# Loading and splitting the per layer input earlier in the second down stage

## The chip, the cores and the metric

The kernel runs on one core of a Trainium2 chip, in one launch. The metric is the time of one execution in device microseconds (us). A core has five engines with queues of their own: TensorE (PE, matmuls, with its weight loads PEld), VectorE (DVE), ScalarE (ACT), GpSimd (POOL) and SyncE (SP). Here SP only issues DMAs, and POOL issues those DMAs that add into a buffer (`accum_op`).

## The reference

```python
for i in range(DEPTH):                                    # 2 layers
    h = h + 0.5 * swiglu(rmsnorm(h, norm_ffn1[i]), ffn1_w_gate[i], ffn1_w_up[i], ffn1_w_down[i])
    hn = rmsnorm(h, norm_mix[i])
    h = h + (ab_mixer(hn, ...) if i % 2 == 0 else c_mixer(hn, ...))
    h = h + 0.5 * swiglu(rmsnorm(h, norm_ffn2[i]), ffn2_w_gate[i], ffn2_w_up[i], ffn2_w_down[i])
    gate = sigmoid(rmsnorm(h, norm_ple[i]) @ w_ple_gate[i])
    h = h + gate * (p[i] @ w_ple_proj[i])                 # per layer input
return rmsnorm(h, norm_final)
```

The sequence has 512 positions, the model 1024 features, the inner width of SwiGLU is 2816, and the per layer input `p[i]` has 512 x 256 values. All are float32.

## The kernel before

Every float32 operand of a matmul is split into a high part and a low part of the type that PE takes: `split` (L153 to L155) lets ACT copy the high part (L154) and DVE subtract it for the low part (L155). A product of two such operands is three matmuls: high by high, high by low, low by high. `split_chunk` splits one 128x512 chunk into two `act` tiles, `parts` a weight buffer `wr` of up to 128x1024 into `wh` and `wl`.

Each layer has two SwiGLU blocks, `ffn(i, 1, ...)` and `ffn(i, 2, ...)`. Each ends with a down stage, `down` (from L493), so there are four in the program; the second one of a layer is followed by the stage of the per layer input, `ple`. A down stage multiplies the 512 x 2816 inner values by the 2816 x 1024 weights with seven block products in place of eight (a scheme of Strassen's kind). In the code the products are called "first" to "seventh", without order of time, and each is cut into six steps s = 0 to 5 along the inner width (step 0 has one unit of 128, the others two). "sixth 3" below is step 3 of the product called sixth. A step of two units is 12 matmuls of 128x512. PE adds up each product in its own PSUM banks: the seventh in `tr` banks, first and sixth in `mm`, second and fourth in `mm` and `ob`, fifth and third in `sc`.

The order of the steps is a list written out by hand (`order`): first a phase of second, first and fifth steps, which ends at index 13; then seventh 0, second 5, first 5, fifth 4, seventh 1, sixth 0, seventh 2, fifth 5, sixth 1, seventh 3, fourth 0, sixth 2, seventh 4, fourth 1, sixth 3, seventh 5, fourth 2, sixth 4, fourth 3, third 0, and so on. For each index the program does four things:

```python
product(*step)          # the matmuls on PE
after(*step)            # what belongs behind this product
ahead(i + LEAD + 1)     # prepare (the splits) four steps ahead, load (DMAs) seven steps ahead
```

`prepare` of a seventh step has DVE add two weight blocks (L566), then ACT and DVE make `wh` and `wl`, and then, in steps 3 to 5, the parts of the inner sums; and it has POOL add a further block to the same buffer by a DMA (L547), which a sixth step reads later, as a fourth step reads what a sixth one left. `load` issues the weights on SP: wide ones into `wr` (5 buffers, L520), narrow ones into `tmp` (10 buffers, L526).

Within this stage the instructions are pinned (`put`): each engine executes them in the order in which they are written. `ffn` hands `down` a function that calls `per_layer` (L478 to L482) twice, once for each half of 128 features: it loads 128x512 values of `p[i]` into a `tmp` buffer by SP (L481) and splits them. `after` calls it behind the product fourth 0 (L653), so the splits stand ahead of the preparation of sixth 3 on ACT and DVE. The four parts are read by `ple`, some 40 us later. In the first down stage of a layer nothing is handed over, and the code is otherwise the same.

Of the kernel before, what the change touches and what calls it, by code (L numbers as in the profile page):

```python
# [56 lines left out]
class Trunk:  # L57
# [92 lines left out]
    def put(self, ins):  # L150
        return self.tc.keep_in_program_order(ins) if self.pinned else ins
# [302 lines left out]
    def ffn(self, i, which, k_next):  # L454


        nc, io = self.nc, self.io
        gu, dn = io[f"gu{which}"][i], io[f"dn{which}"][i]
        first = i == 0 and which == 1
        kept = io["xT"].rearrange("p c t -> c p t") if first else self.put_away()  # L460
        a, sums = [], [None] * K2
        rows, t = self.front(gu, first)
        y = self.xg

        def between():
            a.extend(self.turn_back(rows, self.tbank))
            for k in range(READY):
                if 2 * k + 2 <= len(a) and sums[k] is None:
                    sums[k] = self.inner_sums(*a[2 * k:2 * k + 2])

        for j in range(BLOCKS):
            n = 4 * UNIT + j * 8 * UNIT
            rows = self.block(gu[:, n:n + 8 * UNIT], y, t, between, first and j == 0)
        self.begin_norm(k_next)
        p = lambda: [self.per_layer(i, c) for c in range(2)]
        self.down(dn, a, sums, kept, p if which == 2 else None, lambda n: a.extend(self.turn_back(rows, self.tbank, n)))

    def per_layer(self, i, c):  # L478

        raw = self.tmp()  # L480
        self.nc.sync.dma_start(raw, self.io["pT"][i, :, c, :])  # L481
        return self.split_chunk(raw, self.nc.vector)  # L482

    def inner_sums(self, a, b):

# [7 lines left out]
    def down(self, w, a, sums, kept, inner, turn):  # L493

        nc, H = self.nc, T // 2
# [6 lines left out]
        n = len(units)  # L502
        r1, r2, r3 = [self.bank(), self.bank()], [self.bank(), self.obank()], [self.sbank(), self.sbank()]
        rb = rc = c11 = c5 = c2 = u3 = c21 = None
        x1, x2, x3, x4, raws, more, ops = ({} for _ in range(7))
        put = self.put
# [91 lines left out]
        def copied(p):  # L598
            out = [self.act() for _ in p]
            for o, x in zip(out, p):  # L600
                put(copy(o, x, AF.Copy))
            return out
# [18 lines left out]
        def first_half(m):  # L621
            p, h = self.tbank(), hs[m]
            turned(p[:, l], c11, m)
            turned(p[:, r], c21, m)
            put(nc.vector.scalar_tensor_tensor(h, p, 0.5, h, op0=ALU.mult, op1=ALU.add))
            self.h[m] = h
            floating(self.norm_split, m)

        def second_half(m, x, c):
            p = self.tbank()  # L630
            for j in range(2):
                turned(p[:, j * H:(j + 1) * H], x, m - M + j)
            for j in range(2):
                h = hs[m + j]
                put(nc.vector.scalar_tensor_tensor(h[:, c], p[:, j * H:(j + 1) * H], 0.5, h[:, c], op0=ALU.mult, op1=ALU.add))
                self.h[m + j] = h
            for j in range(2):
                floating(self.norm_split, m + j, c)

        def after(kind, s):  # L640
            nonlocal rb, rc, c11, c5, c2, u3, c21
            if (kind, s) in (("first", 2), ("fifth", 1)):
                turn(range(2) if kind == "first" else range(2, 4))
                if kind == "fifth":
                    rb = [self.tbank(), self.tbank()]
            elif (kind, s) == ("first", 5):
                c11 = copied(r1)
                for o, p in zip(c11, r2):
                    put(tt(o, p, o, op=ALU.add))
                rc = [self.bank(), self.obank()]  # L650
            elif (kind, s) == ("fifth", 5):
                c5 = copied(r3)
            elif (kind, s) == ("fourth", 0) and inner:  # L653
                self.p = inner()
            elif (kind, s) == ("first", 3):
                hs.extend(self.act() for _ in range(KC))
                for m in range(KC):
                    nc.sync.dma_start(hs[m], kept[m])
            elif (kind, s) == ("sixth", 5):
                c2, u3 = copied(r1), [self.act(), self.act()]  # L660
                for i in range(2):
                    put(tt(u3[i], c2[i], rb[i], op=sub))
                for i in range(2):
                    put(tt(c5[i], c5[i], u3[i], op=sub))
            elif (kind, s) == ("fourth", 5):
                c21 = [self.act(), self.act()]
                for i in range(2):
                    put(tt(c21[i], rc[i], u3[i], op=ALU.add))
                second_half(M + 2, c5, r)
            elif (kind, s) == ("third", 2):  # L670
                second_half(M, c5, r)
            elif kind == "third" and 2 < s < 5:
                first_half(2 * s - 6)
                first_half(2 * s - 5)
# [14 lines left out]
        for i, step in enumerate(order):  # L689
            product(*step)  # L690
            after(*step)
            ahead(i + LEAD + 1)
# [941 lines left out]
```

## Time and profile before

| what | us |
|---|---|
| median of 3 runs | 2001.87 (2001.15 to 2005.03) |
| the profiled execution | 2003.01 |
| its span, first to last instruction | 2001.2 |
| matmuls of the second down stage of layer 0 | from 857 to 975 |
| matmuls of the second down stage of layer 1 | from 1815 to 1933 |

The profile shows one execution. Its page gives the busy time of each engine; the views of the trace give each engine's instructions in order of time, with the idle time before them and what ended it, the waits summed up, and the busy time in chosen stretches with the clock that PE was granted (1.00 is full speed). A row of the timeline merges neighbours of one kind (x8). A line such as L154 is that of a helper, so an instruction is recognised by its buffers: `act<-tmp` of L154 is the high part of the per layer input.

### The profile page before, as it was taken

How to read it: one execution, taken by the hardware profiler on the slowest of the kernel's cores; microseconds unless marked ns; L12 is line 12 of the kernel's file. 1: busy time of each engine (PE TensorE's matmuls, PEld its weight loads, DVE VectorE, ACT ScalarE, POOL GpSimd, SP SyncE). 2: the span in 40 equal slices, each digit the busy share in tenths (PEclk: the TensorE clock that was granted, in tenths of full speed). 3: DMA queues.
4: the chain of work that ended last, by engine and by line, in shares of the span. 5: the costliest groups of instructions: out<-in, count | busy, mean ns of one | idle time of the engine just before them, and what ended most of it. 6: DMA issues, size and time to landing. Idle time of an engine off the chain costs nothing.

```text
span 2001.2 us, 28069 instructions
## 1 busy us (share of the span) xinstructions
PE 1974.6 (99%) x9702; PEld 1644.8 (82%) x9702; DVE 1551.5 (78%) x2716; ACT 1218.5 (61%) x2107; POOL 334.7 (17%) x390
## 2 busy tenths in 40 slices
PE   9999999999999999999999999999999999999998
PEld 7888887879888888887888888888888888888786
DVE  8787888698767677787786778887888768678785
ACT  7555656477645555565565556655766556657553
POOL 1111111341211212011122120111000122111111
PEclk9999999999999999999999999999999999999999
DMA  9877697543426777779468785894343577768961
GB/s 275 195 200 163 182 232 229 131 96 80 101 64 226 174 179 183 173 213 252 150 219 184 175 193 153 216 247 150 103 133 101 179 189 189 170 147 229 251 194 42
DMA packets 152223, 348.24 MB, mean 174 GB/s; under 512 B 26512, under 2 KB 34192, under 8 KB 152080
## 3 DMA queue, kind: packets, MB, share of 16 engines
q1 hardware_dynamic: 112128, 235.23, 35.4%
q0 software_dynamic: 39808, 111.17, 31.3%
q8 instruction: 76, 1.25, 0.2%
q14 instruction: 67, 0.55, 0.1%
q10 hardware_dynamic: 144, 0.04, 0.0%
HBM read 318.06 MB, written 17.27 MB: 168 GB/s over the span
## 4 chain that ended last, share of the span: by engine, by line
PE 60%; issue 6%; DVE 6%; DMA 5%; ACT 2%; POOL 1%; SPq 0%; DVEq 0%; POOLq 0%; ACTq 0%
PE mm L179 5%; PE mm L181 5%; PE mm L180 5%; PE mm L595 5%; PE mm L369 4%; PE mm L370 4%; PE mm L368 4%; PE sc L595 3%; DMA wr<-in_gu_dram 3%; PE sc L370 2%; PE sc L369 2%; PE sc L368 2%; DVE wl L155 2%; PE ob L595 2%; PE sc L181 1%
## 5 line engine op out<-in xcount | busy, mean ns | idle before, releaser
L154 ACT ACTIVATE wh<-wr 128x1024 fp32r<-128x1024 f32 (+1 forms) x428 | 438.4, 1029 | 412.1 <-PE mm L370 87.3
L155 DVE TENSOR_TENSOR wl<-wr,wh 128x1024 fp32r<-128x1024 f32 (+1 forms) x428 | 509.8, 1195 | 176.5 <-ACT wh L154 168.0
L368 PE MATMUL mm<-wh,act 128*128 128x512 f32 x640 | 251.0, 392 | 0.0
L370 PE MATMUL mm<-wh,act 128*128 128x512 f32 x640 | 250.8, 392 | 0.0
L369 PE MATMUL mm<-wl,act 128*128 128x512 f32 x640 | 249.5, 390 | 0.1
L179 PE MATMUL mm<-act,wh 128*128 128x512 f32 (+1 forms) x472 | 185.0, 394 | 0.4 <-ACT act L154 0.4
L181 PE MATMUL mm<-act,wl 128*128 128x512 f32 (+1 forms) x472 | 184.6, 392 | 0.0
L180 PE MATMUL mm<-act,wh 128*128 128x512 f32 (+1 forms) x472 | 183.9, 390 | 0.0
L154 ACT ACTIVATE wh<-tmp 128x512 fp32r<-128x512 f32 x248 | 144.9, 623 | 63.8 <-PE sc L370 32.7
L595 PE MATMUL mm<-wh,act 128*128 128x512 f32 x528 | 159.5, 397 | 6.3 <-ACT wh L154 6.3
L155 DVE TENSOR_TENSOR wl<-tmp,wh 128x512 fp32r<-128x512 f32 x248 | 160.5, 684 | 2.9 <-ACT wh L154 2.5
L155 DVE TENSOR_TENSOR act<-act,act 128x512 fp32r<-128x512 f32 (+1 forms) x268 | 141.2, 554 | 3.9 <-ACT act L154 3.7
L338 POOL DMA_DIRECT2D wr<-in_gu_dram x80 | 79.5, 996 | 376.9 <-DVE wl L155 373.4
L369 PEld LDWEIGHTS mm<-wl,act 128*128 128x128 f32 x640 | 120.2, 188 | 24.9 <-DVE wl L155 0.7
L370 PEld LDWEIGHTS mm<-wh,act 128*128 128x128 f32 x640 | 120.2, 188 | 24.4
L368 PEld LDWEIGHTS mm<-wh,act 128*128 128x128 f32 x640 | 120.3, 188 | 23.8
L154 ACT ACTIVATE act<-act 128x512 fp32r<-128x512 f32 (+1 forms) x268 | 125.8, 513 | 15.0 <-DVE act L312 8.3
L368 PE MATMUL sc<-wh,act 128*128 128x512 f32 x320 | 124.7, 390 | 0.5 <-DVE act L292 0.5
L370 PE MATMUL sc<-wh,act 128*128 128x512 f32 x320 | 124.7, 390 | 0.0
L369 PE MATMUL sc<-wl,act 128*128 128x512 f32 x320 | 124.6, 389 | 0.0
L595 PEld LDWEIGHTS mm<-wh,act 128*128 128x128 f32 x528 | 100.3, 190 | 27.9 <-ACT wh L154 7.2
L547 POOL DMA_DIRECT2D wr<-in_dn_dram x72 | 62.3, 880 | 358.4 <-DVE wl L155 352.8
(260 smaller groups left out, 4316.3 us busy)
## 6 DMA issues: line engine op xcount, KB each, us to landing
wr<-in_gu_dram SPq DMA_DIRECT2D x92, 512.0 KB, 4.9
tmp<-in_gu_dram SPq DMA_DIRECT2D x160, 256.0 KB, 3.6
wr<-in_gu_dram POOLq DMA_DIRECT2D x80, 512.0 KB, 7.7
tmp<-in_dn_dram SPq DMA_DIRECT2D x132, 256.0 KB, 6.1
wr<-in_dn_dram POOLq DMA_DIRECT2D x60, 512.0 KB, 7.6
tmp<-in_gu_dram POOLq DMA_DIRECT2D x80, 256.0 KB, 6.0
wr<-in_dn_dram SPq DMA_DIRECT2D x40, 512.0 KB, 5.6
act<-kept SPq DMA_DIRECT2D x56, 256.0 KB, 4.6
```

The lines of the kernel that those rows point to most:

```text
L154: self.put(self.nc.scalar.activation(hi, src, AF.Copy))
L155: self.put((lo_eng or self.nc.vector).tensor_tensor(lo, src, hi.bitcast(F32), op=ALU.subtract))
L179: mm(out, stat[0], mov[0], start=start, stop=False)
L180: mm(out, stat[0], mov[1], start=False, stop=False)
L181: return mm(out, stat[1], mov[0], start=False, stop=stop)
L338: nc.gpsimd.dma_start(raw, q[:, u * UNIT:(u + 1) * UNIT], accum_op=ALU.add)
L368: mm(p, xh, wh, start=start and k == 0, stop=False, skip_group_check=True)
L369: mm(p, xh, wl, start=False, stop=False, skip_group_check=True)
L370: self.last_mm = mm(p, xl, wh, start=False, stop=stop and k == half - 1, skip_group_check=True)
L547: put(nc.gpsimd.dma_start(raw, b[:, u.start * T:u.stop * T], accum_op=ALU.add))
L595: put(nc.tensor.matmul(p, x[k][a][:, c], w[b][:, j * T:(j + 1) * T], start=start and k == a == b == 0, stop=stop and b == 1 and k == u.sto ...
```

## The change

```diff
@@ ffn
         self.begin_norm(k_next)
-        p = lambda: [self.per_layer(i, c) for c in range(2)]
-        self.down(dn, a, sums, kept, p if which == 2 else None, lambda n: a.extend(self.turn_back(rows, self.tbank, n)))
-
-    def per_layer(self, i, c):
-
-        raw = self.tmp()
-        self.nc.sync.dma_start(raw, self.io["pT"][i, :, c, :])
-        return self.split_chunk(raw, self.nc.vector)
+        inner = lambda c: io["pT"][i, :, c, :]
+        self.down(dn, a, sums, kept, inner if which == 2 else None, lambda n: a.extend(self.turn_back(rows, self.tbank, n)))
@@ down, after
             elif (kind, s) == ("fifth", 5):
                 c5 = copied(r3)
-            elif (kind, s) == ("fourth", 0) and inner:
-                self.p = inner()
+            elif (kind, s) == ("fifth", 2) and inner:
+                for c in range(2):
+                    more["inner", c] = self.tmp()
+                    put(nc.sync.dma_start(more["inner", c], inner(c)))
+            elif (kind, s) == ("seventh", 0) and inner:
+                self.p = [self.split_chunk(more.pop(("inner", c)), nc.vector) for c in range(2)]
```

The loads are issued behind the product fifth 2 (index 10) and the splits behind seventh 0 (index 14), where before both stood behind fourth 0 (index 24). The lines behind it move by 6 (the rest of `down`) or 2 (all that follows). The order on PE and on POOL stays as it was; on ACT, DVE and SP these instructions move, in both layers alike. The rows below are of layer 0.

On ACT, ahead of seventh 1 (`wh_8941` before, `wh_8953` now), the program before:

```order
L154 ACTIVATE act_8907<-act_8726 128x512
L154 ACTIVATE wh_8923<-wr_8671 128x1024
L154 ACTIVATE wh_8941<-wr_8872 128x1024
L154 ACTIVATE wh_8958<-wr_8753 128x512
L601 ACTIVATE act_8975<-mm_8481 128x512
```

and the changed one:

```order
L154 ACTIVATE act_8911<-act_8726 128x512
L154 ACTIVATE wh_8927<-wr_8671 128x1024
L154 ACTIVATE act_8943<-tmp_8842 128x512
L154 ACTIVATE act_8947<-tmp_8844 128x512
L154 ACTIVATE wh_8953<-wr_8876 128x1024
L154 ACTIVATE wh_8970<-wr_8753 128x512
L595 ACTIVATE act_8987<-mm_8481 128x512
```

The two splits stand between the `wh` of fifth 4 and that of seventh 1. On DVE their low parts stand in the same way between the `wl` of fifth 4 and the adds of seventh 1.

On ACT, between fourth 1 (`wh_9154`) and sixth 3 (`wh_9182`), the program before:

```order
L154 ACTIVATE wh_9154<-wr_8872 128x1024
L154 ACTIVATE act_9158<-act_7210 128x256
L154 ACTIVATE act_9161<-act_7224 128x256
L154 ACTIVATE act_9172<-tmp_9170 128x512
L154 ACTIVATE act_9178<-tmp_9176 128x512
L154 ACTIVATE wh_9182<-wr_8990 128x1024
L154 ACTIVATE wh_9201<-wr_9130 128x1024
```

and the changed one:

```order
L154 ACTIVATE wh_9166<-wr_8876 128x1024
L154 ACTIVATE act_9170<-act_7210 128x256
L154 ACTIVATE act_9173<-act_7224 128x256
L154 ACTIVATE wh_9182<-wr_9002 128x1024
L154 ACTIVATE wh_9201<-wr_9142 128x1024
```

The splits are gone from here; `wh_9201` is that of seventh 5. On DVE the low parts are gone from the same place.

On SP, the loads before, from the last hidden state (`kept`) over first 5 (`wr_8828`) to seventh 1 (`wr_8872` with two `tmp`):

```order
L658 DMA act_8805<-kept_6550 128x512
L520 DMA wr_8828<-in_dn_dram 128x1024
L520 DMA wr_8872<-in_dn_dram 128x1024
L526 DMA tmp_8874<-in_dn_dram 128x512
L526 DMA tmp_8875<-in_dn_dram 128x512
```

and those of the changed program:

```order
L656 DMA act_8805<-kept_6550 128x512
L514 DMA wr_8828<-in_dn_dram 128x1024
L650 DMA tmp_8842<-in_pT_dram 128x512
L650 DMA tmp_8844<-in_pT_dram 128x512
L514 DMA wr_8876<-in_dn_dram 128x1024
L520 DMA tmp_8878<-in_dn_dram 128x512
L520 DMA tmp_8879<-in_dn_dram 128x512
```

The two loads pass the weights of seventh 1 to seventh 5, which is 15 loads. At the old place, behind seventh 5, the eight `tmp` loads of the third product that follow now stand without them.

## The prediction

> **What bounds the kernel now.** I read the page first, for the share of each engine:
>
> ```profile
> span 2001.2 us, 28069 instructions
> ...
> PE 1974.6 (99%) x9702; PEld 1644.8 (82%) x9702; DVE 1551.5 (78%) x2716; ACT 1218.5 (61%) x2107; POOL 334.7 (17%) x390
> ```
>
> TensorE (PE) is busy for 99% of the span, so only two things can change the time much: an idle PE, or a PE that runs below its clock. Work moved on another engine counts only where PE waits for it. So the second view is the waits of PE, longest first (us in total, times, longest):
>
> ```profile
> PE mm L595 <- ACT wh L154: 6.3, 2, 3.3
> PE tr L1465 <- ACT tmp L1459: 1.6, 1, 1.6
> ```
>
> The largest wait of PE happens twice, in the down matmuls of L595, for a high part `wh` made by ScalarE (ACT) at L154. The third view, the timeline of PE, places it: once in the second down stage of layer 0 and once in that of layer 1. Columns are start, length, what, count, and in brackets the idle time before with its releaser.
>
> ```profile
> 921.54 1.98 PE L595 MATMUL tr<-wh,act 128*128 128x512 f32 x8
> 923.36 1.07 PE L595 MATMUL tr<-wl,act 128*128 128x512 f32 x4
> ...
> 926.76 0.39 PE L595 MATMUL ob<-wl,act 128*128 128x512 f32 x1
> 930.49 2.75 PE L595 MATMUL mm<-wh,act 128*128 128x512 f32 x8 [3.34 <-ACT wh L154]
> ...
> 938.46 0.39 PE L595 MATMUL mm<-wh,act 128*128 128x512 f32 x1
> ...
> 1884.92 0.39 PE L595 MATMUL ob<-wl,act 128*128 128x512 f32 x1
> 1888.32 3.78 PE L595 MATMUL mm<-wh,act 128*128 128x512 f32 x8 [3.00 <-ACT wh L154]
> ...
> 1896.67 0.39 PE L595 MATMUL mm<-wh,act 128*128 128x512 f32 x1
> ```
>
> Two things are to be seen. A group of 8 equal matmuls is followed after 1.82 us (921.54 to 923.36), so one takes 0.227 us. The group of 8 behind the wait takes 2.75 and 3.78 us instead of 1.98: PE is idle first and then slow. The clock is in the windows (after the five busy times: granted clock, DMA share, GB/s):
>
> ```profile
> 920.00:925.00 5.00, 5.00 (x24) 4.14 (x23) 5.00 (x10) 2.62 (x6) 0.87 (x1) 1.00 1.06 300
> ...
> 930.00:935.00 5.00, 4.51 (x13) 3.34 (x14) 3.48 (x5) 2.37 (x4) 0.86 (x1) 0.67 1.04 369
> ...
> 1890.00:1895.00 5.00, 5.00 (x14) 3.91 (x14) 3.74 (x7) 4.10 (x8) 1.54 (x2) 0.57 1.05 329
> ```
>
> Ahead of the wait 24 matmuls go into 5 us at clock 1.00; behind it 13 and 14, at 0.67 and 0.57. So the price of the place is the wait plus the slow stretch. From the start of the product sixth 3 to that of fourth 2 lie two products (sixth 3 and seventh 5), 24 matmuls, 24 x 0.227 = 5.44 us at full rate. The slot of the first was 926.76 + 0.23 = 926.99, and fourth 2 starts at 938.46: 11.47 us, 6.03 too many. In layer 1: 1885.15 to 1896.67 is 11.52, 6.08 too many. **Together 12.1 us**; 3.50 + 3.17 = 6.7 of it idle, 5.4 slow.
>
> Why was ACT late? Its own timeline:
>
> ```profile
> 921.91 0.71 ACT L154 ACTIVATE act<-act 128x256 fp32r<-128x256 f32 x2
> 925.66 0.63 ACT L154 ACTIVATE act<-tmp 128x512 fp32r<-128x512 f32 x1 [3.04 <-DMA tmp<-in_pT_dram]
> 928.86 0.63 ACT L154 ACTIVATE act<-tmp 128x512 fp32r<-128x512 f32 x1 [2.57 <-DMA tmp<-in_pT_dram]
> 929.39 1.04 ACT L154 ACTIVATE wh<-wr 128x1024 fp32r<-128x1024 f32 x1
> ...
> 1884.08 0.63 ACT L154 ACTIVATE act<-tmp 128x512 fp32r<-128x512 f32 x1 [3.77 <-DMA tmp<-in_pT_dram]
> 1886.69 0.63 ACT L154 ACTIVATE act<-tmp 128x512 fp32r<-128x512 f32 x1 [1.98 <-DMA tmp<-in_pT_dram]
> ```
>
> ACT has nothing else to wait for: it is free at 922.6, stands in front of the two splits of the per layer input until 925.66 and 928.86, and only then makes the `wh` that PE waits for. These loads were issued barely before:
>
> ```profile
> 915.61 0.97 SPq L481 DMA_DIRECT2D tmp<-in_pT_dram  x2
> ...
> DMA to landing us min/median/max: 9.3/10.7/12.7
> ```
>
> **The change, part by part.** The instruction count is unchanged: four loads, four ACT and four VectorE (DVE) splits, in two layers, move earlier; PE's and POOL's orders stay.
>
> *Removed from the old place.* ACT's two waits and two splits go (922.6 to 929.4 in layer 0), so `wh` of sixth 3 can be started at 922.6 and is done at 923.7, more than 3 us ahead of its slot at 926.99. The idle time then goes, and, if it caused the slow clock, that too: 12.1 us.
>
> *Is anything else late there?* The first down stage of each layer is the same code without the per layer input. There the same two products run so:
>
> ```profile
> 298.97 1.98 PE L595 MATMUL mm<-wh,act 128*128 128x512 f32 x8
> ...
> 303.67 0.73 PE L595 MATMUL tr<-wh,act 128*128 128x512 f32 x2 [0.20 <-DVE act L155]
> ...
> 305.16 0.39 PE L595 MATMUL mm<-wh,act 128*128 128x512 f32 x1
> ...
> 1321.87 1.98 PE L595 MATMUL mm<-wh,act 128*128 128x512 f32 x8
> ...
> 1327.72 0.40 PE L595 MATMUL mm<-wh,act 128*128 128x512 f32 x1
> ```
>
> 6.19 and 5.85 us instead of 5.44: a loss of 0.75 and 0.41 us in seventh 5, which waits for low parts by DVE (303.67). That is what is late next.
>
> *Added at the new place.* The splits now stand between fifth 4 and seventh 1:
>
> ```profile
> 892.33 1.06 ACT L154 ACTIVATE wh<-wr 128x1024 fp32r<-128x1024 f32 x1 [0.62 <-ACT act L154]
> 896.77 1.58 ACT L154 ACTIVATE wh<-wr 128x1024 fp32r<-128x1024 f32 x2 [3.39 <-DVE wr L566]
> ...
> 1856.13 1.58 ACT L154 ACTIVATE wh<-wr 128x1024 fp32r<-128x1024 f32 x2 [4.32 <-DVE wr L566]
> ```
>
> On ACT two splits of 0.63 fit into idle time of 3.39 and 4.32 us: nothing. DVE has no such gap:
>
> ```profile
> 894.18 1.22 DVE L155 TENSOR_TENSOR wl<-wr,wh 128x1024 fp32r<-128x1024 f32 x1
> 895.32 1.29 DVE L566 TENSOR_TENSOR wr<-wr,tmp 128x512 f32<-128x512 f32 x2
> ...
> 902.50 1.98 PE L595 MATMUL tr<-wh,act 128*128 128x512 f32 x8
> ```
>
> Two low parts of the size of the adds (the pair took 1.29) put off the adds of seventh 1 by up to 1.29 us, and its `wh` from 896.77 to 898.1, done by 899.2; PE wants it at 902.50. So no wait there, but DVE runs nearly without gaps from here on, and carries the delay to seventh 5.
>
> *What the delay costs at seventh 5.* The rows of layer 1:
>
> ```profile
> 1881.94 0.75 DVE L155 TENSOR_TENSOR act<-act,act 128x256 fp32r<-128x256 f32 x2
> ...
> 1889.44 1.29 DVE L566 TENSOR_TENSOR wr<-wr,tmp 128x512 f32<-128x512 f32 x2
> ...
> 1890.90 1.06 ACT L154 ACTIVATE wh<-wr 128x1024 fp32r<-128x1024 f32 x1 [2.63 <-DVE wr L566]
> ...
> 1894.07 0.68 DVE L155 TENSOR_TENSOR act<-act,act 128x512 fp32r<-128x512 f32 x1
> ```
>
> Seventh 5 needs its second low part at its seventh matmul, 6 x 0.227 = 1.36 us in; that part ends 1894.75 - 1890.90 = 3.85 us behind the start of `wh`. In the new program DVE goes on at 1882.69 (plus the delay) with `wl` of sixth 3 (1.15), the adds (1.29), and `wh` starts 0.15 later: 1885.3 without delay, so PE could start at 1885.3 + 3.85 - 1.36 = 1887.8, and it comes at 1885.15 + 2.72 = 1887.87. No wait without delay, 1.2 us with all of 1.29. I take a delay of 1.0 (DVE still has a few gaps of some tenths), so 0.9 us. In layer 0 the same sum from 925.0 gives 930.1 against 929.71: 0.4 us without delay, 1.7 with all. There seventh 4 waits for its transfer anyway,
>
> ```profile
> 917.47 0.69 DVE L566 TENSOR_TENSOR wr<-wr,tmp 128x512 f32<-128x512 f32 x1 [1.35 <-DMA tmp<-in_dn_dram]
> ```
>
> and that gap takes up most of the delay: I take 0.4 of delay, 0.8 us. Both: 1.7 us, between 0.4 and 2.9.
>
> *The loads.* They are issued behind the last load of the first products:
>
> ```profile
> 871.07 6.03 SPq L520 DMA_DIRECT2D wr<-in_dn_dram  x2
> ```
>
> The first of these two issues is at 871.07; the second ends at 877.10, having waited for its buffer. The new loads stand between them, so their 0.97 us of issue falls into a wait and delays nothing. They have from 871.4 to 893.4, 22 us, against 12.7 for the slowest such load. What they hold, two of ten `tmp` buffers for 25 us, costs nothing as the order is built: the weight loads from there up to seventh 5 wait only for a transfer eight places before them, none for a `tmp` buffer. At the old place two later weight loads move up in their stead, so the transfers stay as dense there as before (share 1.06).
>
> **Sum.** 12.1 - 1.7 = 10.4 us less (9.2 to 11.7), against the profiled execution's 2003.01 us (span 2001.2): 1992.6. That execution lies 1.1 above the median of 2001.87, inside the runs' spread. From the median: **1991.5 us**.
>
> **Rivals.**
>
> *The slow clock is not the wait's doing.* For the wait as cause: 0.67 and 0.57 stand right behind the two longest waits, the window ahead has 1.00, and the same products in the first down stages, with little wait, run at full pace. Against: the trace cannot show these two places without the wait. If the slow stretch stayed in both layers, 12.1 - 5.4 - 1.7 = 5.0 us are gained: 1996.9. If only layer 1's stayed (6.08 - 3.17 = 2.9): 1994.4. The Trainium skill, page "TensorE: Matmul & The Clock Gate", section "Part 1: The HAM clock gate (the "warmup" mystery)", says that the array falls to half rate after at least one idle window of about 3.4 us; taken strictly, layer 1's 3.00 us would be too short and its slow stretch would have another cause, which gives the 1994.4. By that rule the trace agrees for layer 0 within a tenth and differs for layer 1, where 3.00 us of idle were followed by 0.57; here the measurement decides. 5%.
>
> *Transfers become the wait.* In favour: share 1.04 to 1.06 of the DMA engines there, and a stage made 5 us shorter wants the same bytes in less time. Against: the first down stages, without the splits, lost only 0.75 and 0.41. If weights land 1 to 2 us later for seventh 5 or fourth 3 in each layer, PE waits 2 to 4 us more in all: 1993.5 to 1995.5. 14%.
>
> *It doesn't do what it says:* the loads are held up and ACT waits at the new place for as long as at the old. Then 2001.9. Against: 22 us of lead. 3%.
>
> *Slower.* Place: ACT in front of `wh` of seventh 1. ACT is in order, so a late load holds everything behind it. PE wants seventh 1 at 902.50, so `wh` has to start by 901.4 and the second load to land by 900.2, 29 us behind its issue. From there each us is a us of PE idle, and from about 3 us of idle on the slow clock comes with it (2.5 to 2.9 us). At 33 us the old price is reached again; at 36 it is 3 us more in each layer, 2008. With 12.7 as the slowest, 2%.
>
> **How the numbers follow.** Forecast 76%; late transfers 14%, clock 5%, no effect 3%, slower 2%. The forecast's own range is 2001.87 - 11.7 = 1990.2 to 1992.7, with about 1 us for a median: 1989 to 1993.5. To hold 8 in 10 with the transfers' case in part: **1989.0 to 1994.5**. A measurement of this kernel tells 0.2%, 4 us, from no change. Faster by more than that takes in the forecast, the transfers and the clock, 95%; 2 of them go to no change, since a clock that stays slow in both layers ends within 1 us of the bound. So faster 0.93, the same 0.05, slower 0.02.
>
> **What would show it.** Right: no wait of ACT for in_pT_dram in the second down stages; no wait of PE for `wh` at L595; the clock at 1.00 across both; sixth 3 to fourth 2 in 5.4 to 6.6 us; ACT's idle time ahead of seventh 1 about 1.2 shorter. Wrong: idle time of PE over 2 us at seventh 5 or later (transfers), a clock below 1.00 without an idle PE ahead of it (clock), or ACT waiting for in_pT_dram ahead of seventh 1 (slower).

## The result and the profile after

| | median us | executions | ratio to before, 95% interval |
|---|---|---|---|
| before | 2001.82 (1998.11 to 2005.03) | 12 | |
| after | 1994.51 (1991.43 to 1998.70) | 12 | 0.9965 [0.9955, 0.9975] |

The change makes the kernel 7.3 us faster, 0.35%. The forecast was 1991.5, 10.4 us less, and its range of 1989.0 to 1994.5 ends just short of the measured median. What was said of the old place came true; the size did not, for losses that the sum had no term for. The profiled execution of after took 1992.47 us, one of the shorter ones, so the pair of profiles shows 10.5 us, more than the medians do.

The page of after, its span and the share of each engine:

```profile
span 1990.7 us, 28067 instructions
...
PE 1969.4 (99%) x9702; PEld 1641.3 (82%) x9702; DVE 1552.9 (78%) x2716; ACT 1220.1 (61%) x2107; POOL 335.0 (17%) x390
```

The waits of PE in after, longest first (us in total, times, longest):

```profile
PE tr L1463 <- ACT tmp L1457: 1.6, 1, 1.6
PE tr L127 <- DVE R L124: 1.3, 1, 1.3
PE tr L608 <- DVE act L629: 1.2, 3, 0.4
```

The largest wait of before, 6.3 us for `wh` in two pieces, has left the list (its line would now be L589). The third row was 0.7 us in two pieces before, both in the first down stages: PE's transposes at the end of a down stage now wait for VectorE (DVE) more often. The timeline of PE in after at the two places, sixth 3, seventh 5 and the start of fourth 2:

```profile
925.32 1.98 PE L589 MATMUL mm<-wh,act 128*128 128x512 f32 x8
...
928.04 2.38 PE L589 MATMUL tr<-wh,act 128*128 128x512 f32 x8
...
931.19 0.39 PE L589 MATMUL mm<-wh,act 128*128 128x512 f32 x1
...
1878.57 1.98 PE L589 MATMUL mm<-wh,act 128*128 128x512 f32 x8
...
1883.41 0.74 PE L589 MATMUL tr<-wh,act 128*128 128x512 f32 x2 [0.20 <-DVE act L155]
...
1884.92 0.39 PE L589 MATMUL mm<-wh,act 128*128 128x512 f32 x1
```

From sixth 3 to fourth 2 it is 5.87 and 6.35 us, 0.43 and 0.91 above the 5.44 of full rate, where before lost 6.03 and 6.08. What is left is the wait for a low part in seventh 5 that the prediction named. The windows behind the places have the clock at 1.00 (0.67 and 0.57 before):

```profile
930.00:935.00 5.00, 5.00 (x23) 4.09 (x22) 5.00 (x9) 3.73 (x8) 0.87 (x1) 1.00 1.05 262
...
1885.00:1890.00 5.00, 5.00 (x24) 4.12 (x23) 4.20 (x8) 2.54 (x6) 0.87 (x1) 1.00 1.05 275
```

But something new stands at the end of the second down stages, in both layers. The timeline of PE in after, its transposes there:

```profile
959.07 0.63 PE L608 MATMUL tr<-ident,act 128*128 128x128 f32 x4 [0.42 <-DVE act L629]
...
962.63 0.66 PE L608 MATMUL tr<-ident,act 128*128 128x128 f32 x4 [0.19 <-DVE act L619]
...
1912.86 0.63 PE L608 MATMUL tr<-ident,act 128*128 128x128 f32 x4 [0.42 <-DVE act L629]
...
1916.43 0.66 PE L608 MATMUL tr<-ident,act 128*128 128x128 f32 x4 [0.17 <-DVE act L619]
```

In the profile of before PE has no such wait in that part of the two stages.

**A ledger of the stage.** PE's order is the same in all these kernels, so a stretch can be counted in matmuls and its time compared from kernel to kernel. Three stretches lose time in the second down stages: (a) the 53 matmuls up to the slot of sixth 3, seventh 4 among them (11.79 us for 52 in layer 0, 12.01 for 53 in layer 1 at full rate); (b) the 25 from there to the start of fourth 2 (5.67 us); (c) the last 74 of layer 0 and 75 of layer 1 (14.88 and 15.09 us, the least that any profile has). The rest of the two stages is equal to within 0.1 us everywhere. Loss in us, layer 0 / layer 1, from the starts of the matmuls in each trace:

| kernel | (a) seventh 4 | (b) sixth 3, seventh 5 | (c) stage end | sum |
|---|---|---|---|---|
| before | 0 / 0 | 6.03 / 6.08 | 0.01 / 0.01 | 12.1 |
| before, second profile (e1) | 0 / 0 | 5.90 / 5.68 | 0 / 0.04 | 11.6 |
| after | 0 / 0 | 0.42 / 0.91 | 0.79 / 0.83 | 3.0 |
| after, second profile (e2) | 0 / 4.00 | 0.07 / 0.33 | 0.77 / 0.43 | 5.6 |
| after, third profile (e13) | 0 / 0.57 | 0.04 / 0.99 | 0.84 / 0.96 | 3.4 |
| e3 loads alone | 0 / 0 | 1.60 / 0.95 | 0.47 / 0.93 | 3.9 |
| e4 splits later | 0 / 0 | 0.06 / 0 | 1.97 / 1.37 | 3.4 |
| e5 before, held | 2.39 / 2.39 | 2.22 / 2.22 | 0.01 / 0.01 | 9.2 |
| e6 after, held | 3.01 / 5.34 | 1.02 / 0.33 | 0 / 0 | 9.7 |
| e7 low parts in a gap | 0 / 0 | 0 / 0 | 0.63 / 0.71 | 1.3 |
| e8 narrow loads first | 0 / 0 | 0.17 / 0 | 0.50 / 0.55 | 1.2 |
| e9 before, narrow loads first in these stages | 0 / 0 | 5.63 / 4.69 | 0.01 / 0.01 | 10.3 |
| e10 after, the same | 0 / 0 | 0 / 0 | 0.56 / 0.47 | 1.0 |
| e11 after, the same in the first stages alone | 0 / 0 | 0.06 / 0.91 | 0.85 / 0.57 | 2.4 |
| e12 both | 0 / 0 | 0 / 0 | 0.01 / 0.04 | 0.1 |
| e14 after, the same for seventh 4 alone | 0 / 0 | 0 / 0.11 | 0.53 / 0.67 | 1.3 |

Two profiles of before lose 11.9 us on average, three of after 4.0: 7.9 us, which is what the medians of all executions give (2001.76 of 93, 1993.94 of 22, on several chips: 7.8). So the change's effect lies in these stages, and the missing 2.5 us too: in columns (a) and (c), for which the forecast had nothing. The rest of the program differs by 2.8 us between the two profiles of before and by 4.1 between those of after, with means 1.1 us apart: scatter, of the size of what is sought. The agreement to 0.1 us is therefore partly luck.

### The profile page after: what moved, and what is told of

Same layout as the page of the kernel before. It is cut to its first block, busy times and chain, and to the rows that moved or that the text cites. A ratio compares the mean times of both kernels' runs of the same rounds, so it can differ in the third digit from the quotient of the medians.

```text
span 1990.7 us, 28067 instructions
## 1 busy us (share of the span) xinstructions
PE 1969.4 (99%) x9702; PEld 1641.3 (82%) x9702; DVE 1552.9 (78%) x2716; ACT 1220.1 (61%) x2107; POOL 335.0 (17%) x390
## 4 chain that ended last, share of the span: by engine, by line
PE 77%; issue 8%; DVE 7%; DMA 4%; ACT 2%; POOL 1%; DVEq 0%; POOLq 0%; ACTq 0%
PE mm L589 7%; PE mm L369 6%; PE mm L368 6%; PE mm L370 6%; PE mm L179 5%; PE mm L181 5%; PE mm L180 5%; PE sc L589 4%; PE sc L368 3%; PE sc L370 3%; PE sc L369 3%; DVE wl L155 3%; PE ob L589 2%; DMA wr<-in_gu_dram 2%; PE tr L589 2%
## 5 line engine op out<-in xcount | busy, mean ns | idle before, releaser
L589 PE MATMUL mm<-wh,act 128*128 128x512 f32 x528 | 156.9, 391 | 0.0
L589 PEld LDWEIGHTS mm<-wh,act 128*128 128x128 f32 x528 | 99.1, 188 | 20.4
```

The lines of the kernel that those rows point to most:

```text
L589: put(nc.tensor.matmul(p, x[k][a][:, c], w[b][:, j * T:(j + 1) * T], start=start and k == a == b == 0, stop=stop and b == 1 and k == u.sto ...
```

## The experiments

**Twice the same, e1 and e2.** The kernel before and the changed one, unedited, for a second profile of each.

> The kernel before, unchanged, for a second profile. In the first profile the place (sixth 3 to fourth 2) lost 6.03 us in layer 0 and 6.08 in layer 1. Theory A (the profile was a usual execution): again 11 to 13 us over both layers, the clock at half for 3 to 7 us in each. Theory B (the size of the loss changes from one execution to the next, which is why the medians differ by 7.3 us where the profiles differ by 10.5): 8 to 10 us over both layers, with less slow clock. Time between 1998 and 2005 us.

> The changed kernel, unchanged, for a second profile. In its first profile (1992.5 us) the place lost 0.43 + 0.91 us and the end of the stage 1.3 us. Theory A (as the first profile): the same within 1 us, and a time of 1992 to 1995. Theory C (some executions have a further loss of 3 to 6 us that the first profile does not show, since three of twelve took 1998.5 to 1998.7): where this execution is above 1996 its profile shows an idle or slow PE of that size somewhere else. No wait of ScalarE for the per layer input under any theory.

Measured: before 2003.25 us (11 executions), ratio 1.0008 [0.9999, 1.0017]; after 1994.21 (5), ratio 0.9962 [0.9948, 0.9976]. Both profiles taught something. In that of before, the timeline of PE in layer 0 shows the same wait, but another rate behind it:

```profile
930.38 2.11 PE L595 MATMUL mm<-wh,act 128*128 128x512 f32 x8 [3.21 <-ACT wh L154]
...
934.59 2.07 PE L595 MATMUL tr<-wh,act 128*128 128x512 f32 x6 [1.19 <-ACT act L154]
...
938.35 0.39 PE L595 MATMUL mm<-wh,act 128*128 128x512 f32 x1
```

and the window has the clock at 1.00:

```profile
930.00:935.00 5.00, 3.43 (x14) 2.47 (x14) 3.48 (x5) 2.37 (x5) 0.87 (x1) 1.00 1.05 364
```

No slow stretch here, and yet the place lost 5.90 us instead of 6.03: PE ran sixth 3 at full rate and then stood 1.19 us more, waiting for the parts of seventh 5, which ScalarE (ACT) and VectorE make behind the same late splits. The slow clock in the first profile had mostly filled time that PE would have waited. (In layer 1 of e1 the clock did fall, to 0.66 from 1890 to 1895, and the place lost 5.68 us.) So "6.7 idle and 5.4 slow" were not two prices that add up; the place was set by the chain of ACT and VectorE behind the late load.

The profile of after, at 1999.21 us the longest of its five executions, shows what the first one did not have, at seventh 4 of layer 1. On DVE the second add of that step waits for its narrow load (`tmp`):

```profile
1874.31 0.69 DVE L560 TENSOR_TENSOR wr<-wr,tmp 128x512 f32<-128x512 f32 x1 [0.44 <-DMA tmp<-in_dn_dram]
1877.03 0.69 DVE L560 TENSOR_TENSOR wr<-wr,tmp 128x512 f32<-128x512 f32 x1 [2.03 <-DMA tmp<-in_dn_dram]
```

and on PE sixth 2, seventh 4 and the start of fourth 1:

```profile
1874.54 1.98 PE L589 MATMUL mm<-wh,act 128*128 128x512 f32 x8
...
1879.52 3.67 PE L589 MATMUL tr<-wh,act 128*128 128x512 f32 x8 [2.10 <-ACT act L154]
...
1883.95 0.39 PE L589 MATMUL mm<-wh,act 128*128 128x512 f32 x1
```

9.41 us for 24 matmuls instead of 5.44: 2.10 idle, and the group of 8 slow behind it. The two narrow loads were issued together:

```profile
1864.50 1.06 SPq L520 DMA_DIRECT2D tmp<-in_dn_dram  x2
```

so the later one landed some 12 us behind its issue. Of the 22 executions of after in all, 4 lie between 1998.5 and 1999.2, and the other 18 between 1991.3 and 1995.3.

**One half of the change each, e3 and e4.** e3 keeps the early loads and leaves the splits at the old place; e4 keeps the loads at the old place and puts the splits later.

```diff
 (e3)
-            elif (kind, s) == ("seventh", 0) and inner:
+            elif (kind, s) == ("fourth", 0) and inner:
                 self.p = [self.split_chunk(...)]
 (e4)
-            elif (kind, s) == ("fifth", 2) and inner:
+            elif (kind, s) == ("fourth", 0) and inner:
                 for c in range(2): ...
-            elif (kind, s) == ("seventh", 0) and inner:
+            elif (kind, s) == ("third", 0) and inner:
                 self.p = [self.split_chunk(...)]
```

> The loads issued behind fifth 2 as in the changed kernel, the splits left behind fourth 0 as in the kernel before. Theory 1 (ScalarE waited for late loads, the splits themselves are cheap): no wait of ScalarE for the per layer input, clock 1.00, the place loses 2.5 to 3.5 us over both layers since the two low parts (1.29 us) stand right ahead of sixth 3 and seventh 5 on VectorE; time 1 to 2 us above the changed kernel. Rival 2 (it is the place of the splits that counts): the place still loses over 8 us, time as before.

> The loads issued behind fourth 0 as in the kernel before, the splits put off to behind third 0, some 22 us later. Theory 1: no wait for the loads, no split ahead of seventh 5, so the place loses only what the first down stages lose (0.4 to 0.8 us in each layer), clock 1.00; at the end of the stage VectorE has 1.29 us more to do than in the changed kernel, so the waits of TensorE for the last additions grow from 1.3 us to 1.5 to 3 over both layers; time within 1.5 us of the changed kernel. Rival 2 (early loads are what counts): ScalarE still waits for the loads, at third 2, by 2 us or more.

Measured: e3 1995.22 us (7 executions), 0.9971 [0.9961, 0.9982]; e4 1996.47 (11), 0.9971 [0.9962, 0.9980]. Either half keeps most of the gain, and in neither does ACT wait for the per layer input: the price of before was ACT and DVE standing in front of loads that had just been issued, and not the splits' work. What differs is where DVE's work comes out (columns b and c). In e3 it comes out at seventh 5, from the timelines of DVE and, below it, of PE in layer 0:

```profile
917.95 0.69 DVE L560 TENSOR_TENSOR wr<-wr,tmp 128x512 f32<-128x512 f32 x1 [1.25 <-DMA tmp<-in_dn_dram]
...
925.40 1.29 DVE L155 TENSOR_TENSOR act<-tmp,act 128x512 fp32r<-128x512 f32 x2
```

```profile
930.83 2.08 PE L589 MATMUL tr<-wh,act 128*128 128x512 f32 x6 [0.39 <-ACT act L154]
933.11 0.73 PE L589 MATMUL tr<-wh,act 128*128 128x512 f32 x2 [0.20 <-DVE act L155]
```

In e4 nothing is lost there, and the end of the stage pays, on PE's timeline:

```profile
961.28 0.33 PE L608 MATMUL tr<-ident,act 128*128 128x128 f32 x1 [0.48 <-DVE act L666]
961.88 0.33 PE L608 MATMUL tr<-ident,act 128*128 128x128 f32 x1 [0.27 <-DVE act L666]
962.63 0.63 PE L608 MATMUL tr<-ident,act 128*128 128x128 f32 x4 [0.42 <-DVE act L629]
...
966.20 0.66 PE L608 MATMUL tr<-ident,act 128*128 128x128 f32 x4 [0.19 <-DVE act L619]
```

1.97 us against 0.79 in after: the two low parts, 1.29 us of DVE, come out almost whole. Two expectations were missed: the place lost less than the 0.4 to 0.8 us in each layer, and the median is 2.3 us above that of after in e2, on the same chip, where 1.5 was the limit. The ledger of the one profile, 3.4 us, doesn't show why. From here the theory was: with PE's pause gone, DVE has no slack left from seventh 1 to the stage's end, and a delay of DVE, from splits or from a late load, reaches PE. It holds up to seventh 5; what sets the stage's end in after is another thing, shown further below.

**A delay of one size in both kernels, e5 and e6.** Six adds on a spent buffer, 4.2 us of DVE by their rows (3.6 in the expectation), between the two adds of seventh 4 in the second down stages.

```diff
                     put(tt(z, z, y, op=ALU.add))
+                    if inner and s == 4 and j == 0:
+                        for _ in range(6):
+                            put(tt(y, y, y, op=ALU.add))
```

> The kernel before, with six extra VectorE adds of 128x512 (0.6 us each, on a spent buffer) between the two adds of seventh 4, in the second down stage of both layers: 3.6 us of VectorE, as if that step's second narrow load landed late. Theory 'the old wait took up such delays': ACT and VectorE stand waiting for the per layer input until 925.66 and 928.86 anyway, so seventh 4 comes about 3 us late on PE and sixth 3 not at all: within 1 us of the kernel before in all (2001 to 2003.5). Rival 'a late load costs the same in both kernels': 3 us and more in each layer, 2008 or later.

> The changed kernel with the same six adds in both layers. Theory: nothing behind takes up the delay now. Seventh 4 has a slack of about 0.4 us on VectorE (in the run that lost 4.0 us in layer 1 VectorE was held 2.5 us and PE idled 2.10), so about 3.2 us of PE idle in each layer, with or without a slow clock behind it (up to 2.9 each): 2000 to 2006, all of the change's gain. Rival 'slack elsewhere takes it up': within 2 us of the changed kernel, 1994 to 1996.

Measured: e5 2000.61 us (11), ratio 0.9994 [0.9985, 1.0003]; e6 2000.32 us (11), ratio 0.9996 [0.9987, 1.0004]. The delay costs the kernel before nothing that can be measured, and takes from the changed one all of its gain, some 6 us. The held kernels lose nothing at the stage end, either of them (column c). PE's timeline in e5, layer 0: the wait of 3.34 us has become two of about 1 us, at seventh 4 and seventh 5, and the wait for the per layer input is gone because its loads had time to land:

```profile
922.05 2.08 PE L598 MATMUL tr<-wh,act 128*128 128x512 f32 x6 [1.18 <-ACT act L154]
...
932.43 2.07 PE L598 MATMUL tr<-wh,act 128*128 128x512 f32 x6 [1.00 <-ACT act L154]
```

And in e6, both layers:

```profile
922.78 2.07 PE L592 MATMUL tr<-wh,act 128*128 128x512 f32 x6 [1.80 <-ACT act L154]
...
1880.57 3.67 PE L592 MATMUL tr<-wh,act 128*128 128x512 f32 x8 [3.44 <-ACT act L154]
```

e6 lies in the theory's band; e5 is within 1 us of before on its chip, 0.4 below the band in figures. In layer 0 of e6 the idle time was 1.80 us instead of 3.2; why is not shown.

**DVE's backlog, e7.** The low parts go behind the adds of seventh 1, where DVE waits 1.26 us for ACT's `wh` anyway.

```diff
-            elif (kind, s) == ("seventh", 0) and inner:
-                self.p = [self.split_chunk(more.pop(("inner", c)), nc.vector) for c in range(2)]
@@ prepare, seventh
+                if inner and s == 1:
+                    self.p = [(self.act(F32R), self.act(F32R)) for c in range(2)]
+                    for c in range(2):
+                        put(copy(self.p[c][0], more["inner", c], AF.Copy))
                 for j, y in enumerate(more.pop(s)):
                     ...
+                if inner and s == 1:
+                    for c in range(2):
+                        put(tt(self.p[c][1], more.pop(("inner", c)), self.p[c][0].bitcast(F32), op=sub))
                 w, x = self.parts(raws[n + s]), x3
```

> The changed kernel, with the two low parts of the per layer input on VectorE behind the adds of seventh 1, where VectorE waits 1.26 us for ScalarE's wh of that step in any case; the two high parts stay ahead of that wh on ScalarE. Theory 'VectorE's backlog is carried to seventh 5 and to the stage end': 1.3 us less backlog, so the losses at seventh 5 (0.43 and 0.91) go to 0.1 to 0.4 each and those at the end of the stage (0.79 and 0.81) to 0.3 or less: 1 to 2.5 us faster than the changed kernel, 1992 to 1993.4. Rival 'the stage end loses by something else, the transposes' own order': no change there, under 0.7 us gained in all.

Measured: 1992.33 us (5 executions, 1990.12 to 1992.45), ratio 0.9952 [0.9939, 0.9964]. Seventh 5 loses nothing any more (0.42 and 0.91 in after). The stage end fell only to 0.63 and 0.71, more than the 0.3 expected. So the splits account for the loss at seventh 5, and for a small part of that at the end.

**The transfers, e8.** The narrow loads of a seventh step are issued ahead of its wide one, which waits for a buffer on SP and holds them up.

```diff
-                raws[n + s], more[s] = wide(b12, u), narrow(b22, u)
+                more[s], raws[n + s] = narrow(b22, u), wide(b12, u)
```

> The changed kernel, with the two narrow loads of each seventh step issued ahead of its wide one instead of behind it, in all four down stages. In the run of the changed kernel that lost 4.0 us at seventh 4 of layer 1, the second narrow load landed some 12 us behind its issue. Theory 'some executions lose about 4 us to that late load': the narrow loads are issued some 4 us or more earlier, the executions above 1998 (4 of 17 so far) are gone, the median falls by 0.5 to 1.5 us, and no wait of DVE for tmp is seen at seventh 4. Rival 'only the order of two loads on a full set of DMA engines changes': the wide one is late in its place, same spread and median.

Measured: 1989.90 us (5 executions, 1989.51 to 1990.87), ratio 0.9943 [0.9930, 0.9955]: about 4 us faster than after (3 against e13, on the same chip), more than the 0.5 to 1.5 expected, no wait of DVE for a narrow load, and a spread of 1.4 us. The edit acts in all four down stages, and both kernels share the first ones. Hence the next three, one per kind of stage and kernel.

**Which stages, e9 to e11.** The edit of e8 under `if inner:` (second down stages), in the kernel before (e9) and the changed one (e10), and under `if not inner:` (first down stages) in the changed one (e11).

> The kernel before, with the narrow loads of the seventh steps issued ahead of the wide ones in the second down stages alone. Theory 'the old wait for the per layer input took up late narrow loads': nothing is gained, since sixth 3 waits for the per layer input as before: ratio 0.9985 to 1.0005, 1999 to 2003. Rival 'late narrow loads cost the same in both kernels': as much faster as the changed kernel becomes by the same edit.

> The changed kernel with the same edit, in the second down stages alone. Theory: late narrow loads for seventh 4 are where the rest of the forecast gain goes. 2 to 3.5 us faster than the changed kernel, 1991 to 1992.5, and none of the executions above 1997. Rival 'the 4.5 us that the edit gained in all four stages lie in the first down stages, which both kernels share': 1994 to 1995.

> The changed kernel with the same edit in the first down stage of each layer alone. Theory: 1 to 2.5 us faster than the changed kernel, 1992 to 1993.5, a gain that has nothing to do with the change under study, and single executions above 1997 are still there. Rival 'the 4.5 us lie in the first down stages': 1990 to 1990.5.

| | median us | executions | ratio to before |
|---|---|---|---|
| e9 before, second stages | 2002.58 | 12 | 1.0003 [0.9994, 1.0012] |
| e10 after, second stages | 1991.59 (1989.94 to 1994.61) | 5 | 0.9950 [0.9938, 0.9962] |
| e11 after, first stages | 1991.60 (1990.97 to 1994.10) | 5 | 0.9951 [0.9939, 0.9963] |

In the second down stages the edit gains the kernel before nothing and the changed one about 2.4 to 2.9 us by the medians. (In the profile of e9 sixth 3 no longer waits, against what was expected; the wait has moved on by one product, to 3.73 and 2.80 us ahead of seventh 5.) With it the changed kernel is 10.2 us ahead of before, and 11.0 ahead of e9, the size that was forecast. The first stages hold a gain of like size (somewhat more than expected), which has nothing to do with the change. No execution of e11 lies above 1997, where some were expected; with five executions that says little. The intervals of e10 and of after overlap between 0.9955 and 0.9962, so the size of the 2.4 to 2.9 us is loose.

**Both edits, e12.** e7 and e8 together.

> Both edits that beat the changed kernel: the low parts of the per layer input in VectorE's gap behind the adds of seventh 1, and the narrow loads ahead of the wide ones in all four down stages. If the two losses are apart (VectorE's backlog, transfers): 1 to 2 us faster than the narrow loads alone, 1988 to 1989. If both worked on the same wait: 1989.5 to 1990.5.

Measured: 1989.80 us (5 executions, 1988.59 to 1990.63), ratio 0.9939 [0.9927, 0.9951]. By the time it can't be told from e8, and it lies in the band given for one common wait, 1989.5 to 1990.5. The profile speaks for two: it has no loss left in the second down stages. (This execution was the longest of the five; it is 2.0 us longer than that of e8 outside these stages.) The low parts stand in the gap on DVE, whose next instruction no longer waits,

```profile
894.08 1.29 DVE L564 TENSOR_TENSOR wr<-wr,tmp 128x512 f32<-128x512 f32 x2
895.28 1.29 DVE L567 TENSOR_TENSOR act<-tmp,act 128x512 fp32r<-128x512 f32 x2
896.63 1.83 DVE L155 TENSOR_TENSOR wl<-wr,wh 128x1024 fp32r<-128x1024 f32 x2
```

and sixth 3, seventh 5 and fourth 2 of layer 1 follow one another at full rate, 5.44 us, on PE:

```profile
1878.35 1.98 PE L596 MATMUL mm<-wh,act 128*128 128x512 f32 x8
...
1881.07 1.98 PE L596 MATMUL tr<-wh,act 128*128 128x512 f32 x8
...
1883.79 0.39 PE L596 MATMUL mm<-wh,act 128*128 128x512 f32 x1
```

Of the stage end's loss either edit alone left 1.0 to 1.3 us, both together 0.05. e8 and e12 are the fastest versions, both ahead of the two kernels of the study.

**One step alone, e13 and e14.** The changed kernel a third time, and beside it the edit of e8 for seventh 4 of the second down stages alone (`if inner and s == 4`).

> The changed kernel itself, once more, beside the next one on one chip. Theory: median 1994 to 1995, some executions above 1997; whether this profile has a late load at seventh 4 is a matter of chance (one of two so far).

> The changed kernel, with the narrow loads ahead of the wide one for seventh 4 alone, in the second down stages alone: one step in each layer. Theory 'the rest of the forecast gain is lost to the late narrow load of this step': as fast as with all steps of the second down stages, 1991 to 1992.5, 2 to 3 us faster than the changed kernel on this chip. Rival 'it is lost over many steps': at most 1 us faster, 1993.5 or later.

Measured: e13 1993.02 us (5, 1991.32 to 1994.60), ratio 0.9954 [0.9941, 0.9966]; e14 1992.25 (5, 1991.77 to 1996.28), 0.9956 [0.9942, 0.9970]. None of these five executions of after lies above 1995, and its median came out below the 1994 expected. The difference of 0.8 is what the rival gave (at most 1 us), the time of e14 what the theory gave, so this pair decides nothing; one execution of e14 still took 1996.28. That seventh 4 alone is the place in most of the late executions stays open; that it can be is shown by e2.

## Why the prediction was right in kind and off in size

**Right.** ACT no longer waits for the per layer input anywhere; the wait of PE for `wh` is gone in both layers; the clock is at 1.00 across both places; sixth 3 to fourth 2 takes 5.87 and 6.35 us, inside the 5.4 to 6.6 given. The loads were early enough. On the low parts ahead of seventh 1 the forecast was right that they carry to seventh 5: 1.7 us were set down (0.4 to 2.9), three profiles show 1.3, 0.4 and 1.0, and without them in DVE's way (e7) 0. In layer 0 the gap of 1.35 us ahead of seventh 4 did take up the delay: it is gone in all three profiles of after, and seventh 5 lost 0.42, 0.07 and 0.04 us there. One sign was read wrongly: ACT's idle time ahead of seventh 1 did not become 1.2 shorter. The timeline of ACT in after has

```profile
896.52 1.58 ACT L154 ACTIVATE wh<-wr 128x1024 fp32r<-128x1024 f32 x2 [3.76 <-DVE wr L560]
```

where before had 3.39, because ACT then waits for DVE's adds, which stand behind the low parts.

**The sum at the old place** (12.1 us) was right, its split into 6.7 idle and 5.4 slow was not. e1 lost 5.90 us in layer 0 with no slow stretch at all. What a slow clock without the wait would cost was not tested: no profile has one there. The rule of the Trainium skill that the prediction weighed, about 3.4 us of idle ahead of half rate (page "TensorE: Matmul & The Clock Gate", Part 1), doesn't sort these waits: behind 3.34, 3.00 and 2.10 us the clock fell, behind 3.21 it did not. The last section shows what does.

**The step that failed** is the sum. It has a term for seventh 5 and none for seventh 4 or for what comes behind, and it puts the transfers at nothing ("the transfers stay as dense there as before"). "What is late next" was read from the first down stages between sixth 3 and fourth 2 alone, and late transfers became a rival of 14%. The runs show two losses there instead:

- *The stage end*, 1.6, 1.2 and 1.8 us for the two layers in three profiles of after, 0.05 or less in those of before and in e5, e6 and e9. On average 1.5 us of the missing 2.5. It comes from a transfer and not from the low parts on DVE. POOL issues the load that adds to the weights of fourth 4 as soon as DVE has read that buffer for sixth 4, and ACT then waits for it. The rows of POOL and ACT in layer 0 of before, and of POOL, ACT and DVE in after:

```profile
941.16 0.87 POOL L547 DMA_DIRECT2D wr<-in_dn_dram  x1 [4.62 <-DVE wl L155]
946.75 1.06 ACT L154 ACTIVATE wh<-wr 128x1024 fp32r<-128x1024 f32 x1 [1.79 <-DMA wr<-in_dn_dram]
```

```profile
933.87 0.87 POOL L541 DMA_DIRECT2D wr<-in_dn_dram  x1 [4.62 <-DVE wl L155]
942.46 1.06 ACT L154 ACTIVATE wh<-wr 128x1024 fp32r<-128x1024 f32 x1 [3.03 <-DMA wr<-in_dn_dram]
943.55 1.23 DVE L155 TENSOR_TENSOR wl<-wr,wh 128x1024 fp32r<-128x1024 f32 x1 [2.65 <-ACT wh L154]
```

Fourth 2 starts on PE at 938.46 and 931.19, so the load is issued 2.7 us behind it in both kernels: DVE is no further behind in after, and it even stands idle for 2.65 us. But the load lands after 5.5 us in before and after 8.5 in after, and this `wh` starts 8.3 and 11.3 us behind fourth 2. In the second down stages of all 16 profiles that distance sets the loss: none up to 10.4 us, above that the distance less 10.5, to within 0.1 (1.3 more in e4, where the two low parts stand behind it). What PE's old pause gave was time for the transfers: while this load was under way the DMA engines had a share of 0.91 in before (940 to 945) and 1.07 in after (935 to 940). e6, with a pause in the changed kernel, has the load land after 5.5 and 5.3 us and loses nothing; e12 issues it 0.9 us earlier, and 8.4 us are soon enough. In the profile of before the same loss stood in the first down stages, which have no per layer input to split, on PE's timeline:

```profile
332.94 0.63 PE L614 MATMUL tr<-ident,act 128*128 128x128 f32 x4 [0.37 <-DVE act L635]
...
1355.45 0.63 PE L614 MATMUL tr<-ident,act 128*128 128x128 f32 x4 [0.29 <-DVE act L635]
```

Counted as in column (c) this is 0.59 and 0.50 us, with the same load landing after 8.4 and 8.3 us.

- *A late start of seventh 4.* Where DVE waits for a load, the load just misses, and there is no reserve against a later one. In before, what such a load costs PE is taken off the wait that follows: e5 showed it with 4.2 us of DVE work that cost nothing, e9 by gaining nothing. In after it costs in full: e6 (6 us), e2 (4.0 us in one layer). Three profiles of after lost 0, 4.0 and 0.6 in column (a), on average another 1.5 us, with wide scatter. Only the 4.0 is a late narrow load: in e13 DVE waits for none and starts its adds 3.6 us ahead of PE's seventh 4, against 4.3 in the first profile.

Against these stand 0.8 us that seventh 5 lost less than forecast (1.7 to 0.9) and 0.2 us that before lost less in its second profile: 10.4 - 1.5 - 1.5 + 0.8 - 0.2 = 8.0, against 7.9 from the profiles and 7.3 to 7.8 from the medians. The rival "transfers become the wait" named this effect and a time of 1993.5 to 1995.5, where the median lies, but put it at seventh 5 or fourth 3, where the runs have seventh 4 and fourth 4. It was taken for the less likely case, from first down stages that "lost only 0.75 and 0.41"; e11 shows that those too lose about 2.4 us by the median.

**Chance.** Single executions scatter by a few us, in stages that both kernels share too: the profile of before lay 1.2 above its median and that of after 2.0 below, so that the pair agreed with the forecast better than the medians did. With three profiles of after, and two of before, the terms and the medians meet, in part by luck: one of the three is as long as only 4 of the 22 executions are.

## What to carry to other kernels

A wait that ends last also hides every smaller delay ahead of it: before you count its full length as gain, add up what the engines and the transfers behind it still owe, to the end of the stage and not to the next wait, and look for it in stages that never had the wait. An engine seen waiting for a transfer off the critical path isn't idle reserve; it is the next bound, and its price can be tested by holding both kernels back by the same amount. Where loads share one queue, put those that need no buffer ahead of one that waits for a buffer: here that was worth about half of the change under study.

## What the hardware showed that was not expected

- The clock behind an idle PE. The length of a wait doesn't say whether the clock falls: it did behind 3.34 and 3.00 us (before), 3.44 (e6, layer 1) and 2.10 (e2), and not behind 3.21 (e1, layer 0) and 1.80 (e6, layer 0). Where the wait lies does. In the clock records of each trace the clock changes only at instants a whole number of 3.41 us apart. A window between two such instants and the one that follows it are shown here for layer 0 of before, layer 0 of e1 and layer 1 of e2 (after the length, the first figure is PE's busy time; the clock stands before the DMA share):

```profile
928.32:931.73 3.41, 1.24 (x5) 1.05 (x6) 1.96 (x3) 1.58 (x2) 0.00 (x0) 1.00 1.06 409
931.73:935.15 3.42, 3.42 (x9) 2.44 (x8) 2.16 (x3) 2.08 (x4) 0.86 (x1) 0.50 1.01 338
```

```profile
928.62:932.04 3.42, 1.66 (x7) 1.40 (x8) 2.37 (x3) 1.58 (x2) 0.16 (x1) 1.00 1.06 409
932.04:935.45 3.41, 2.22 (x10) 1.37 (x9) 2.15 (x4) 2.49 (x5) 0.70 (x1) 1.00 1.06 319
```

```profile
1876.10:1879.51 3.41, 1.32 (x6) 0.75 (x4) 1.22 (x2) 1.62 (x3) 0.00 (x0) 1.00 1.05 324
1879.51:1882.92 3.41, 3.40 (x8) 2.73 (x9) 3.41 (x8) 3.41 (x7) 0.87 (x1) 0.50 1.03 291
```

The clock falls to 0.50 where PE was idle for most of the window before (2.17 and 2.09 us here), and stays at 1.00 where it was idle for less (1.76 here, because an instant splits the 3.21 us). In all 16 traces, between the first 20 us and the last 30, seven windows had 2.09 to 3.41 us of idle PE and all were followed by the slow clock; none with up to 1.76 us was, unless the clock was slow already. Between 1.76 and 2.09 there is no case.

- A narrow load of 128x512, one of a pair, landed some 12 us behind its issue in e2, while its like in layer 1 of the first profile of after landed 9.2 us behind its issue at 1860.2, 0.1 us ahead of the add that reads it. With the DMA engines at a share of 1.05 such a spread decides between no loss and 4 us.
